# Four changes in the order of ScalarE's work in a fused attention and RG-LRU step

## The chip, the cores and the metric

The kernel runs on one core of a Trainium2 chip. A core has five engines that each work through a queue of their own, in the order in which the program wrote it: TensorE (PE) multiplies matrices, VectorE (DVE) and ScalarE (ACT) work element by element, so does GpSimd (POOL), and SyncE (SP) starts DMAs. An engine that has to wait for another stands still, and so does everything queued behind that instruction. The metric is the device time of one execution in microseconds (us).

## The reference, cut to what matters

One layer with two groups of heads that read the same normalised and modulated input, for 128 context tokens and 1024 latent tokens (1152 columns in all), model width 1024:

```python
h = rms_norm(x, g_pre) * (1.0 + scale) + shift          # shift, scale, gate = silu(c) @ w_ada + b_ada
p = h @ w_in
q, k, v, g_att, x_lru, g_lru = jnp.split(p, SPLITS, axis=-1)
q, k = axial_rope(q), axial_rope(k)                      # latent tokens only
o = diff_attention(q, k_all, v_all, lam)                 # 8 heads, two softmax maps per head
att = (rms_norm(o, g_subln) * (1.0 - lam_init)) * jax.nn.silu(g_att)
u = centred_conv(x_lru, conv_w, conv_b)
hf = linear_scan(a_f, b_f, h0_f, False)                  # a, b from two gates of u
hb = linear_scan(a_b, b_b, h0_b, True)
lru = (hf + hb) * jax.nn.silu(g_lru)
out = jnp.concatenate([att, lru], axis=-1) @ w_out
x_new = x + gate * rms_norm(out, g_post)
```

It returns both new token sets, the new keys and values, and the final states of the recurrence. Inputs and outputs are fp32.

## The kernel before, in words

**How a product is made.** An fp32 product is three products of 16-bit (or reduced fp32) halves, lines 119 to 121: high by high, low by high, high by low. Whatever TensorE multiplies must first be split: a cast or a scaled copy on ScalarE makes the high half, and an operation on VectorE (or GpSimd) subtracts it from the original and leaves the low half. For weights these are `whi` (line 314, ScalarE) and `wlo` (line 324, VectorE), for the input `hTh` (line 495) and `hTl` (line 116), for a head's queries and keys `hlq` and `hlk` (lines 931 and 932), for values lines 1021 and 1022, for the output weights `woh` (line 222, ScalarE) and `wol` (line 113, half of them on VectorE and half on GpSimd). Before a tensor is split it is scaled by a power of two; for a weight block that is `wunit` (squares on ScalarE at line 290, a sum over the partitions by TensorE at line 297, the power of two by VectorE at lines 194 to 199), and for a head `qksc` (squares on ScalarE at line 907, the sum by TensorE at line 918, the power of two at line 194 again).

**The stages.** Up to about 82 us the modulation is computed: sixteen pieces of `w_ada` in four groups A, B, C, D of four. `mod` multiplies one piece (line 434), `mod_rows` copies a group's result to SBUF on ScalarE (line 439), and `mod_turn` transposes it on TensorE (line 444). Groups A and B give scale and shift for the first half of the model's width (tiles 0 to 3 of the eight tiles of x), C and D for the second half (tiles 4 to 7). `unit_h`, `scales`, `bounds` and `shares` are small VectorE operations that make the factors `sc` and `sh` of a half. `normed` multiplies a tile by its norm (line 483), `modulate` applies scale and shift and casts to `hTh` (lines 492 and 495 on ScalarE; with `hi=V` lines 489 and 497 on VectorE), `h_lo` makes `hTl`. The first block of `w_in` is multiplied while this goes on: `first_chunk(k)` for tiles 0 to 3 into one set of accumulators, tiles 4 to 7 into another (`x0b`). From 82 to 410 us eight blocks of the recurrence run, from 410 to 706 us the heads' queries, keys and values with their gates, from 706 to 730 us the last gates, and from there to the end attention, with the products by `w_out` (`po`) between its tiles.

**What sets the order.** Each engine's order is the order in which the code was written. Blocks of heads are written by `qk_block` (line 897): for each of three column chunks `j` the product and its copy to SBUF on ScalarE (`qk_chunk`, line 764), and then `tick()`. `after(n, step)` puts a step off by n ticks, so that the later steps of one head (`power`, the sum and power of two; `turned`, the rotary embedding on VectorE at lines 891 to 894; `halves`, lines 931 and 932; `send`, the DMAs) are written between the chunks of the next. `squares` (line 907) is not put off: it is written behind the tick of the last chunk. `v_block` does the same for values; its copies are at line 983 and its halves at line 1021. `g_block` (line 1096 on) writes a gate: three chunks, three sigmoids (line 732), three products (line 738). The last gate is that of head 7. Four pieces of `w_out` and their splits are put off to ticks inside it; the second four loads into the same four buffers (`wor`) are put off too.

Of the kernel before, what the change touches and what calls it, by code (L numbers as in the profile page):

```python
# [29 lines left out]
NCH = T // CH  # L30
# [67 lines left out]
def hybrid_step_kernel(ctx: ExitStack, tc: tile.TileContext, io):  # L98
# [148 lines left out]
    with ExitStack() as pa:  # L247
# [118 lines left out]
        with ExitStack() as stp:  # L366
# [10 lines left out]

            xt = [sp.tile([P, T], F32, name=f"xt{k}") for k in range(KT)]
            what = {"A": (0, 1), "B": (0, 0), "C": (1, 1), "D": (1, 0)}
            for x in "A0 A1 w A2 A3 x0 x1 B0 x2 x3 B1 x4 x5 B2 x6 x7 B3 C0 C1 C2 C3 D0 D1 D2 D3 w w w".split():  # L380
                if x == "w":
                    w_load()
                elif x[0] == "x":
                    k = int(x[1])
                    nc.sync.dma_start(out=xt[k], in_=io["xT"][:, k])
                else:
                    load_wa(*what[x[0]], int(x[1]))
# [43 lines left out]
            def mod(half, part, b):  # L431
                raw = wa.pop((half, part, b))
                for i in range(2):
                    PE.matmul(modps[half, part][0:2], lhsT=cs[:, 2 * b + i], rhs=raw[:, i], start=b == 0 and i == 0,
                              stop=b == 3 and i == 1)

            def mod_rows(half, part):
                rows = modr[half, part] = sw.tile([2, 512], F32, tag="rows", name=f"rows{half}{part}", bufs=2)
                S.copy(out=rows, in_=modps[half, part][0:2])

            def mod_turn(half, part):
                t4 = ssq[:, 16:24].rearrange("p (i c) -> p i c", i=4)
                for i in range(4):
                    PE.transpose(t4[:, i], modr[half, part][:, i * P:(i + 1) * P], ident[0:2, 0:2])
                kk = part * 8 + half * 4
                V.tensor_tensor(out=modT[:, kk:kk + 4], in0=t4,
                                in1=vec[:, ba + kk:ba + kk + 4].unsqueeze(2).to_broadcast([P, 4, 2]), op=ALU.add)
# [38 lines left out]
            def modulate(k, eng=V, hi=S):  # L486
                for w, a, b in ((1, 0, CTX), (0, CTX, T)):
                    if eng is V:
                        V.tensor_scalar(out=xt[k][:, a:b], in0=xt[k][:, a:b], scalar1=sc1[:, w, k:k + 1],
                                        scalar2=sh1[:, w, k:k + 1], op0=ALU.mult, op1=ALU.add)  # L490
                    else:
                        S.activation(out=xt[k][:, a:b], in_=xt[k][:, a:b], func=AF.Identity, scale=sc1[:, w, k:k + 1],
                                     bias=sh1[:, w, k:k + 1])
                if hi is S:
                    S.copy(out=hTh[k], in_=xt[k])
                else:
                    V.tensor_copy(out=hTh[k], in_=xt[k])

            def h_lo(k):
                split_lo16(V, hTl[k], xt[k], hTh[k])  # L500
# [42 lines left out]
            normed(1)  # L543
            modulate(0, S)
            mod(*C, 3)
            modulate(1, S)
            normed(2)
            h_lo(0)
            mod_rows(*C)
            normed(3)  # L550
            mod(*D_, 0)
            modulate(2, S)
            h_lo(1)
            mod_turn(*C)
            for b in range(1, 4):
                mod(*D_, b)
            normed(4)
            modulate(3, S)
# [12 lines left out]
                for j in range(NCH):  # L571
                    chunk(accs[j] if k < 4 else accb[:, j], 16, 0, j, [k], k % 4 == 0, k % 4 == 3)

            for k in range(2):
                first_chunk(k)
            mod_turn(*D_)
            scales(1)
            bounds(1)
            unit_h(1)
            shares()  # L580
            for k in range(2, 4):
                first_chunk(k)
            modulate(4, S)
            modulate(6, hi=V)
            h_lo(6)
            w_back(1)
            h_lo(4)
            modulate(5, S)
            one = w_hi()
            modulate(7, hi=V)  # L590
            h_lo(7)
            h_lo(5)
            w_lo(one)
            for x, k in enumerate((4, 6, 7, 5)):
                for j in range(NCH):
                    chunk(accb[:, j], 16, 0, j, [k], x == 0, x == 3)
            w_square()
# [299 lines left out]
        def qk_block(which, h):  # L897
# [52 lines left out]
            if not first:  # L950
                for j in range(NCH):
                    qk_chunk(which, h, t_, j)
                    tick()
            if which or h > 1:
                squares()
                if which:
                    after(1, context_keys)
                for x, step in zip((1, 1, 3, 4), steps[1:]):
                    after(x, step)
            else:  # L960

                for x, step in zip(((5, 7, 8, 10, 11), (7, 9, 10, 12, 13))[h], steps):
                    after(x - 3 * h, step)
# [159 lines left out]
        load_lt(0, 0)  # L1123
        for kt in GROUPS[0]:
            load_wo(kt, 0)
        after(2, lambda: [split_wo(kt, 0, V if kt % 2 else G) for kt in GROUPS[0][:2]])
        after(3, lambda: [split_wo(kt, 0, V if kt % 2 else G) for kt in GROUPS[0][2:]])
        after(3, lambda: [load_wo(kt, 1) for kt in GROUPS[0]])
        assert len(AMONG) + 2 == NH
        g_block(gp_, NH - 1)  # L1130
        for n in range(2, 4):
            load_q(n)
        for t in range(1, 3):
# [569 lines left out]
```

## Time and profile before

| | |
|---|---|
| three runs | 1256.38, 1257.6, 1251.76 us; median 1256.38 us |
| profiled execution | 1255.92 us, span of its trace 1254.1 us |
| TensorE busy | 1141.9 us, 91% of the span |
| VectorE busy | 1033.5 us, 82% |
| ScalarE busy | 786.9 us, 63% |
| GpSimd busy | 302.1 us, 24% |
| chain that ended last, by engine | VectorE 36%, TensorE 36%, ScalarE 10%, DMA 7%, issue 7%, GpSimd 3% |

The span is the stretch that the trace covers; the execution's own time is 1.82 us longer. "Busy" counts time in which at least one instruction of the engine ran, so a product that runs at half clock counts for more. The chain is followed back from the last instruction: at each step to what released it.

### The profile page before, as it was taken

The numbers are of one execution on the slowest core, as the hardware profiler recorded it, in microseconds if no ns is written. First come the engines' busy times: TensorE is split into PE (matmuls) and PEld (weight loads), VectorE is DVE, ScalarE is ACT, GpSimd is POOL, SyncE is SP. The second block draws the span as 40 slices with busy tenths as digits, with TensorE's granted clock in tenths as the row PEclk, the third lists the DMA queues.
The fourth block names the chain that finished last, engine by engine and source line by source line (L and its number), as shares of the span: only waits on it lengthen the run. The fifth ranks groups of instructions, "written<-read, shape, count | busy, mean of one in ns | idle before, by whom it ended". The sixth has DMA issues, their size and how long they took to land.

```text
span 1254.1 us, 20667 instructions
## 1 busy us (share of the span) xinstructions
PE 1141.9 (91%) x7804; PEld 786.2 (63%) x7804; DVE 1033.5 (82%) x1880; ACT 786.9 (63%) x1330; POOL 302.1 (24%) x172
## 2 busy tenths in 40 slices
PE   6889999999999899899899969988989888999887
PEld 1346666666666755675766747766767665666675
DVE  5686898889887988867868547899898989999877
ACT  4457577657766555545445347877877786777632
POOL 0000000000000000000000013346965686667624
PEclk8889999999999999899899989999999999999999
DMA  9311322231223345625534276999888998899954
GB/s 363 142 43 43 116 70 73 91 116 61 81 91 105 98 116 172 167 73 151 152 102 91 78 242 133 212 207 231 189 209 187 230 225 176 200 205 223 197 205 159
DMA packets 277819, 188.76 MB, mean 151 GB/s; under 512 B 196172, under 2 KB 246092, under 8 KB 276952
## 3 DMA queue, kind: packets, MB, share of 16 engines
q1 hardware_dynamic: 277432, 186.60, 56.1%
q8 instruction: 61, 1.00, 0.3%
q10 hardware_dynamic: 288, 0.85, 0.2%
q14 instruction: 38, 0.31, 0.1%
HBM read 102.20 MB, written 46.94 MB: 119 GB/s over the span
## 4 chain that ended last, share of the span: by engine, by line
DVE 36%; PE 36%; ACT 10%; DMA 7%; issue 7%; POOL 3%; SPq 1%; DVEq 0%; ACTq 0%; POOLq 0%
DVE mx L1231 6%; DVE e L1259 5%; DVE wlo L324 3%; PE s L1222 2%; PE s L1224 2%; PE ga L119 2%; POOL a L1263 2%; PE v L119 2%; PE v L120 2%; PE v L121 2%; PE ga L120 2%; PE ga L121 2%; ACT e L1241 2%; PE po L119 2%; PE po L120 1%
## 5 line engine op out<-in xcount | busy, mean ns | idle before, releaser
L1241 ACT ACTIVATE e<-s,mx,back 128x1152 f32<-128x1152 f32 (+1 forms) x144 | 175.5, 1219 | 64.6 <-DVE mx L1237 16.9
L113 POOL TENSOR_TENSOR wol<-wor,woh 128x512 fp32r<-128x512 f32 x24 | 33.4, 1393 | 683.9 <-ACT woh L222 683.8
L1263 POOL TENSOR_TENSOR a<-e,a 128x1152 f16<-128x1152 f32 (+1 forms) x72 | 157.9, 2193 | 166.6 <-ACT a L1262 158.3
L1231 DVE TENSOR_REDUCE mx<-s 128x1 f32<-128x1152 f32 (+1 forms) x144 | 177.3, 1231 | 21.0 <-PE s L1224 20.1
L119 PEld LDWEIGHTS <-whi 128*128 128x128 f16 x960 | 96.6, 101 | 63.6 <-issue 6.4
L121 PEld LDWEIGHTS <-wlo 128*128 128x128 f16 x960 | 94.1, 98 | 65.4 <-issue 3.7
L120 PEld LDWEIGHTS <-whi 128*128 128x128 f16 x960 | 94.2, 98 | 64.1 <-issue 7.2
L1222 PE MATMUL s<-kt,qt 128*128 128x384 f16 (+1 forms) x400 | 88.0, 324 | 42.4 <-ACT e L1241 40.4
L1259 DVE SCALAR_TENSOR_TENSOR e<-e,fa,e 128x1152 f32<-128x1152 f32 (+1 forms) x72 | 114.3, 1587 | 6.4
L119 PE MATMUL po<-woh,lt 128*128 128x512 f32 x216 | 98.7, 457 | 12.8 <-DVE sg L738 7.1
L119 PE MATMUL pv<-vt,t 128*128 128x128 f16 x584 | 103.2, 221 | 3.1 <-ACT ot L1278 2.5
L120 PE MATMUL pv<-vt,t 128*128 128x128 f16 x584 | 102.7, 220 | 0.0
L121 PE MATMUL pv<-vt,t 128*128 128x128 f16 x584 | 102.6, 220 | 0.0
L1262 ACT CAST a<-e 128x1152 f16<-128x1152 f32 (+1 forms) x72 | 75.8, 1053 | 37.1 <-DVE e L1259 23.9
L1224 PE MATMUL s<-kt,qt 128*128 128x384 f16 (+1 forms) x400 | 87.8, 325 | 0.0
L121 PE MATMUL po<-woh,lt 128*128 128x512 f32 x216 | 86.3, 400 | 0.0
L120 PE MATMUL po<-wol,lt 128*128 128x512 f32 x216 | 85.8, 397 | 0.0
L119 PE MATMUL v<-whi,hTh 128*128 128x256 f16 x288 | 81.6, 283 | 3.2 <-DVE qksc L194 2.3
L120 PE MATMUL v<-wlo,hTh 128*128 128x256 f16 x288 | 81.6, 283 | 0.0
L121 PE MATMUL v<-whi,hTl 128*128 128x256 f16 x288 | 81.4, 282 | 0.0
L1222 PEld LDWEIGHTS <-qt 128*128 128x128 f16 x400 | 33.6, 97 | 71.4 <-issue 59.3
L324 DVE SCALAR_TENSOR_TENSOR wlo<-wraw,wboth,whi 128x512 f16<-128x512 f32 x94 | 66.2, 746 | 12.7 <-ACT whi L314 12.4
(361 smaller groups left out, 3242.7 us busy)
## 6 DMA issues: line engine op xcount, KB each, us to landing
wraw<-in_w_in_dram SPq DMA_DIRECT2D x48, 512.0 KB, 3.6
lt<-mix SPq DMA_DIRECT2D x27, 512.0 KB, 4.1
qs<-hlq SPq DMA_DIRECT2D x64, 144.0 KB, 3.1
qt<-qs SPq DMA_DIRECT2D x72, 128.0 KB, 3.5
wa<-in_w_ada_dram SPq DMA_DIRECT2D x16, 512.0 KB, 10.6
wor<-in_w_out_dram SPq DMA_DIRECT2D x32, 256.0 KB, 3.7
mix<-amo SPq DMA_DIRECT2D x6, 1152.0 KB, 5.8
vs<-v SPq DMA_DIRECT2D x8, 640.0 KB, 2.9
```

Of the source, the lines that this page charges most:

```text
L113: eng.tensor_tensor(out=lo, in0=val, in1=f(hi), op=ALU.subtract)
L119: PE.matmul(out, lhsT=lh, rhs=rh, start=start, stop=False)
L120: PE.matmul(out, lhsT=lh, rhs=rl, start=False, stop=False)
L121: PE.matmul(out, lhsT=ll, rhs=rh, start=False, stop=stop)
L324: V.scalar_tensor_tensor(out=lo[:, i % 2, r], in0=raws[i][:, r], scalar=wboth[:, i, x:x + 1], in1=hi[:, i % 2, r], op0=ALU.mult, op1=ALU.s ...
L1222: PE.matmul(sps[:, j, :w_], lhsT=qt[:, mp], rhs=kt_[:, mp, c], start=True, stop=False)
L1224: PE.matmul(sps[:, j, :w_], lhsT=qt[:, 2 + mp], rhs=kt_[:, mp, c], start=False, stop=True)
L1231: V.tensor_reduce(out=d["mx"][:, mp:mp + 1], in_=sv, axis=AX.XY, op=ALU.max, negate=True)
L1241: S.activation(out=e_[:, :nk].rearrange("p (j c) -> p j c", c=w_), in_=sv, func=AF.Exp, bias=d["mx"][:, mp:mp + 1], scale=unit, accum_out= ...
L1259: V.scalar_tensor_tensor(out=e1, in0=e1, scalar=d["fa"], in1=e0, op0=ALU.mult, op1=ALU.subtract)
L1262: S.copy(out=a16[:, 0:nk], in_=e1)
L1263: G.tensor_tensor(out=a16[:, nk:2 * nk], in0=e1, in1=a16[:, 0:nk], op=ALU.subtract)
```

## The change

Four things are written in another order, and one cast changes its engine.

- The DMAs of x and of group B's weights: each of B1, B2 and B3 is ahead of one tile of x more than before, and B0 ahead of x1.
- Before the first block: group C's rows are copied ahead of `modulate(1)`, not behind it; `mod(D,1)` stands ahead of C's transpose on TensorE; only tile 0's chunk stands ahead of D's transpose (tiles 0 and 1 before); tile 6 is written ahead of tile 4, the cast of tile 7 moves from VectorE to ScalarE, and the chunks of the second half run in the order 6, 4, 7, 5.
- Squares of a head: `squares` is called between the last chunk's copy and its tick, which is ahead of whatever that tick writes: the halves of the head before, or of two values.
- The last gate: the splits of the first four pieces of `w_out` and the loads of the second four are written behind the gate's sigmoids and products.

```diff
--- before.py
+++ after.py
@@ -377,7 +377,7 @@
 
             xt = [sp.tile([P, T], F32, name=f"xt{k}") for k in range(KT)]
             what = {"A": (0, 1), "B": (0, 0), "C": (1, 1), "D": (1, 0)}
-            for x in "A0 A1 w A2 A3 x0 x1 B0 x2 x3 B1 x4 x5 B2 x6 x7 B3 C0 C1 C2 C3 D0 D1 D2 D3 w w w".split():
+            for x in "A0 A1 w A2 A3 x0 B0 x1 x2 B1 x3 x4 B2 x5 x6 B3 x7 C0 C1 C2 C3 D0 D1 D2 D3 w w w".split():
                 if x == "w":
                     w_load()
                 elif x[0] == "x":
@@ -543,16 +543,17 @@
             normed(1)
             modulate(0, S)
             mod(*C, 3)
+            mod_rows(*C)
             modulate(1, S)
             normed(2)
             h_lo(0)
-            mod_rows(*C)
             normed(3)
             mod(*D_, 0)
             modulate(2, S)
             h_lo(1)
+            mod(*D_, 1)
             mod_turn(*C)
-            for b in range(1, 4):
+            for b in range(2, 4):
                 mod(*D_, b)
             normed(4)
             modulate(3, S)
@@ -571,27 +572,26 @@
                 for j in range(NCH):
                     chunk(accs[j] if k < 4 else accb[:, j], 16, 0, j, [k], k % 4 == 0, k % 4 == 3)
 
-            for k in range(2):
-                first_chunk(k)
+            first_chunk(0)
             mod_turn(*D_)
             scales(1)
             bounds(1)
             unit_h(1)
             shares()
-            for k in range(2, 4):
+            for k in range(1, 4):
                 first_chunk(k)
+            modulate(6, hi=V)
             modulate(4, S)
-            modulate(6, hi=V)
             h_lo(6)
-            w_back(1)
+            modulate(7)
             h_lo(4)
             modulate(5, S)
+            w_back(1)
+            h_lo(7)
             one = w_hi()
-            modulate(7, hi=V)
-            h_lo(7)
             h_lo(5)
             w_lo(one)
-            for x, k in enumerate((4, 6, 7, 5)):
+            for x, k in enumerate((6, 4, 7, 5)):
                 for j in range(NCH):
                     chunk(accb[:, j], 16, 0, j, [k], x == 0, x == 3)
             w_square()
@@ -950,9 +950,10 @@
             if not first:
                 for j in range(NCH):
                     qk_chunk(which, h, t_, j)
+                    if j == NCH - 1 and (which or h > 1):
+                        squares()
                     tick()
             if which or h > 1:
-                squares()
                 if which:
                     after(1, context_keys)
                 for x, step in zip((1, 1, 3, 4), steps[1:]):
@@ -1123,11 +1124,12 @@
         load_lt(0, 0)
         for kt in GROUPS[0]:
             load_wo(kt, 0)
-        after(2, lambda: [split_wo(kt, 0, V if kt % 2 else G) for kt in GROUPS[0][:2]])
-        after(3, lambda: [split_wo(kt, 0, V if kt % 2 else G) for kt in GROUPS[0][2:]])
-        after(3, lambda: [load_wo(kt, 1) for kt in GROUPS[0]])
         assert len(AMONG) + 2 == NH
         g_block(gp_, NH - 1)
+        for kt in GROUPS[0]:
+            split_wo(kt, 0, V if kt % 2 else G)
+        for kt in GROUPS[0]:
+            load_wo(kt, 1)
         for n in range(2, 4):
             load_q(n)
         for t in range(1, 3):
```

ScalarE before the first block, the difference (`rows` is the copy of a modulation group, `hTh` the cast high half of a tile, numbers are buffers):

```order
 L495 CAST hTh_131<-xt_157 128x1152
+L439 COPY rows_383<-modpA 2x512
 L492 ACTIVATE xt_158<-xt_158,sh_117,sc_116 128x128
 L492 ACTIVATE xt_158<-xt_158,sh_117,sc_116 128x1024
 L495 CAST hTh_132<-xt_158 128x1152
-L439 COPY rows_388<-modpA 2x512
 L492 ACTIVATE xt_159<-xt_159,sh_117,sc_116 128x128
 L492 ACTIVATE xt_159<-xt_159,sh_117,sc_116 128x1024
```

The copy of group C's rows has moved up past one tile's two activations and its cast. Further down the queue the cast of tile 7 has come in between the cast of tile 4 and the activations of tile 5.

ScalarE at the end of a key block, before (`qfk_4584` is the block just multiplied, `qfk_4458` the one before it, `wjunk` the squares):

```order
L764 ACTIVATE qfk_4584<-k_1_4667,winv 128x384
L764 ACTIVATE qfk_4584<-k_2_4693,winv 128x384
L931 ACTIVATE hlk_4719<-qfk_4458,qksc 128x1280
L907 ACTIVATE wjunk,sqk_4722<-qfk_4584 128x1280
L983 ACTIVATE vf_0_4724<-v_0_4729,winv 128x128
```

and the same place now:

```order
L764 ACTIVATE qfk_4584<-k_1_4667,winv 128x384
L764 ACTIVATE qfk_4584<-k_2_4693,winv 128x384
L907 ACTIVATE wjunk,sqk_4719<-qfk_4584 128x1280
L931 ACTIVATE hlk_4721<-qfk_4458,qksc 128x1280
L984 ACTIVATE vf_0_4724<-v_0_4729,winv 128x128
```

The squares of the new block and the high half of the block before it have changed places; this happens at thirteen ends of blocks, and at three of them two value halves (line 1021, 1022 now) stand between as well.

ScalarE at the last gate, before (`woh` casts of `w_out`, `sg` the gate's sigmoids):

```order
L222 CAST woh_0_6925<-wor_0_6867 128x512
L222 CAST woh_0_6929<-wor_0_6869 128x512
L222 CAST woh_0_6958<-wor_0_6871 128x512
L222 CAST woh_0_6962<-wor_0_6873 128x512
L732 ACTIVATE sg_6974<-ga_0_6875,winv 128x384
L732 ACTIVATE sg_6974<-ga_1_6900,winv 128x384
L732 ACTIVATE sg_6974<-ga_2_6933,winv 128x384
L222 CAST woh_1_6991<-wor_1_6966 128x512
L222 CAST woh_1_6995<-wor_1_6968 128x512
```

and now:

```order
L732 ACTIVATE sg_6950<-ga_0_6875,winv 128x384
L732 ACTIVATE sg_6950<-ga_1_6900,winv 128x384
L732 ACTIVATE sg_6950<-ga_2_6925,winv 128x384
L222 CAST woh_0_6957<-wor_0_6867 128x512
L222 CAST woh_0_6961<-wor_0_6869 128x512
L222 CAST woh_0_6965<-wor_0_6871 128x512
L222 CAST woh_0_6969<-wor_0_6873 128x512
L222 CAST woh_1_6991<-wor_1_6973 128x512
L222 CAST woh_1_6995<-wor_1_6975 128x512
```

The three sigmoids stand ahead of the first four casts; the second four casts stay where they were behind them. On VectorE the gate's three products have moved up past two `wol` in the same way.

## Rows read from the trace of the kernel before

**Rows 1.** Stretches: us, busy PE, PEld, DVE, ACT, POOL (instructions), PE clock, DMA share, GB/s.

```profile
0.00:45.00 45.00, 35.09 (x100) 9.75 (x100) 23.35 (x73) 16.74 (x19) 1.05 (x11) 0.89 0.93 352
45.00:82.00 37.00, 28.01 (x123) 12.74 (x122) 29.41 (x63) 22.98 (x32) 0.34 (x6) 0.82 0.04 15
82.00:410.00 328.00, 324.31 (x1982) 213.73 (x1981) 279.21 (x435) 224.07 (x286) 0.00 (x0) 1.00 0.26 83
```

**Rows 2.** TensorE before first block: start, duration, operation, [idle <-releaser].

```profile
49.42 0.58 PE L444 MATMUL ssq<-ident,rows 2*128 2x2 f32 x4 [3.95 <-ACT rows L439]
...
69.46 0.48 PE L120 MATMUL x0b<-hTl,whi 128*128 128x384 f16 x1 [2.58 <-DVE hTl L116]
...
77.86 0.28 PE L297 MATMUL ssq<-wsq,onesf 128*128 128x1 f32 x2
```

**Rows 3.** ScalarE before the first block.

```profile
57.55 0.57 ACT L439 COPY rows<-modpB 2x512 f32<-2x512 f32 x1 [1.71 <-PE modpB L434]
63.70 1.63 ACT L492 ACTIVATE xt<-xt,sh,sc 128x128 f32<-128x128 f32 x2 [5.57 <-DVE sh L471]
65.35 1.15 ACT L495 CAST hTh<-xt 128x1152 f16<-128x1152 f32 x1
```

**Rows 4.** VectorE before the first block.

```profile
64.50 1.06 DVE L489 TENSOR_SCALAR xt<-xt,sc,sh 128x128 f32<-128x128 f32 x2
65.60 0.76 DVE L497 CAST hTh<-xt 128x1152 f16<-128x1152 f32 x1
66.39 1.36 DVE L116 TENSOR_TENSOR hTl<-xt,hTh 128x1152 f16<-128x1152 f32 x1
```

**Rows 5.** Three stretches at half clock, columns as in rows 1.

```profile
68.19:75.02 6.83, 5.56 (x18) 2.60 (x18) 6.76 (x8) 4.45 (x7) 0.00 (x0) 0.50 0.00 0
522.16:528.99 6.83, 6.04 (x29) 4.42 (x30) 6.16 (x22) 3.93 (x11) 0.00 (x0) 0.50 0.42 126
733.79:740.61 6.82, 3.10 (x7) 2.48 (x8) 4.75 (x6) 4.50 (x9) 3.81 (x3) 0.50 0.74 232
```

**Rows 6.** Who waited for the squares of line 907 (us, times).

```profile
  PE unk L918: 9.8, 3
```

**Rows 7.** TensorE at two kinds of pause among the heads.

```profile
522.95 0.58 PE L918 MATMUL unk<-sqk,onesf 128*128 128x1 f32 x2 [4.28 <-ACT wjunk L907]
...
591.28 0.32 PE L119 MATMUL k<-hTh,whi 128*128 128x384 f16 x1 [1.75 <-DVE wunit L194]
```

**Rows 8.** ScalarE ahead of the first of these pauses.

```profile
520.28 1.36 ACT L931 ACTIVATE hlk<-qfk,qksc 128x1280 f16<-128x1280 f32 x1 [3.90 <-DVE qfk L894]
521.55 1.25 ACT L907 ACTIVATE wjunk<-qfk 128x1280 bf16<-128x1280 f32 x1
```

**Rows 9.** One round of two blocks, columns as in rows 1.

```profile
518.50:589.50 71.00, 66.42 (x459) 46.34 (x458) 53.36 (x124) 35.67 (x65) 0.00 (x0) 0.95 0.40 119
```

**Rows 10.** VectorE in that round, first and last of five such pauses.

```profile
542.57 0.54 DVE L973 TENSOR_REDUCE vmx<-vf 128x1 f32<-128x128 f32 x2 [0.80 <-ACT vf L983]
...
555.60 0.16 DVE L1013 COPY sgv<-vmu 128x2 f32<-128x2 f32 x1 [0.59 <-PE vmu L1012]
```

**Rows 11.** TensorE between last gate and attention.

```profile
737.51 0.79 PE L119 MATMUL po<-woh,lt 128*128 128x512 f32 x1 [7.05 <-DVE sg L738]
...
743.34 0.65 PE L1222 MATMUL s<-kt,qt 128*128 128x384 f16 x3 [1.24 <-ACT e L1241]
```

**Rows 12.** ScalarE there.

```profile
730.51 1.32 ACT L222 CAST woh<-wor 128x512 fp32r<-128x512 f32 x2 [10.14 <-DMA wor<-in_w_out_dram]
...
734.58 1.51 ACT L732 ACTIVATE sg<-ga,winv 128x384 f32<-128x384 f32 x3
...
741.44 1.28 ACT L1241 ACT_TABLE_LOAD   x1 [1.82 <-DVE mx L1234]
```

**Rows 13.** VectorE there.

```profile
735.80 1.66 DVE L738 SCALAR_TENSOR_TENSOR sg<-ga,winv,sg 128x384 f32<-128x384 f32 x3
```

## The prediction

> **What bounds the kernel now.** I read the page's busy shares first, and then one row for each stage, because no engine is the bound throughout. From 82 to 410 us TensorE is busy for 324.31 of 328.00 us [rows 1]: what comes earlier into that stage leaves it earlier by as much, and nothing there is touched. Before it, from 45 to 82 us, TensorE is busy for 28.01 of 37.00 us at a mean clock of 0.82, so pauses and slow products are both to be had. I then looked in TensorE's timeline for pauses that end on ScalarE or on something that ScalarE holds up. There are three kinds in the places that the change touches. Before the first block TensorE waits 3.95 us for the copy of group C's rows and later 2.58 us for the low half of a tile [rows 2]. Among the heads it waits for the squares: 9.8 us in three pauses for keys [rows 6], one of them 4.28 us at 522.95 [rows 7]. Between the last gate and attention it waits 7.05 us for the gate's products [rows 11].
>
> A pause costs more than its length. The granted clock is 0.50, which is 1.2 GHz of 2.4, from 522.16 to 528.99 around the end of the 4.28 us pause, and from 733.79 to 740.61 at the end of the 7.05 us one [rows 5]. A pause of the second kind, shorter and ended by VectorE, is that at 591.28: 1.75 us for the power of two of a weight block [rows 7].
>
> **The change part by part.**
>
> *Loads.* Three pieces of B come one tile of x (128 x 1152 fp32, 0.59 MB) earlier. At the 352 GB/s of the first 45 us [rows 1] that is 1.7 us, and it can't help by more; at worst, since the tiles of x come later by a piece of B (0.52 MB), it costs 1.5 us. What follows needs both, so most of it cancels; I take −0.4 us.
>
> *Modulation.* The copy of group C's rows passes one tile's activations and cast, 1.63 and 1.15 us [rows 3], and a piece of D stands ahead of the transpose, so the pause of 3.95 us goes. What is late next is ScalarE itself: the copy of D's rows waited 1.71 us for TensorE [rows 3], so this copy can come 1.71 us earlier and no more. Behind it only tile 0's nine products stand ahead of D's transpose. At half clock 18 products of this shape took 5.56 us [rows 5], so nine take 2.8 us, and at full clock 1.4 us. I count the half clock here, and let the factors of the second half of the model's width be ready 1.35 us earlier than at 63.70 [rows 3], that is at 62.35.
>
> *Second half.* VectorE's queue decides from there. It began 0.80 us after the factors (64.50 against 63.70) [rows 3, 4]. Now it has tile 6's modulation and cast, tile 7's modulation, and four low halves: 1.06 + 0.76 + 1.06 + 4 x 1.36 = 8.3 us [rows 4], with about 1.3 us for the weight's small operations and hand-overs. The last low half is there at 62.35 + 0.80 + 8.3 + 1.3 = 72.8 us, and the nine products behind it end at 74.2 if the clock is full. Before, the step behind these products began at 77.86 [rows 2]: −3.6 us. The cast of tile 7 leaves VectorE's queue and costs ScalarE 1.15 us [rows 3], beside work of VectorE. If the clock falls, all 36 products of the half take twice as long, and if ScalarE's extra cast delays tile 5, another 1.15 us is lost, so the ends are −5 and 0.
>
> The Trainium skill (ScalarE: Activation LUTs, section Rules for kernel authors) says that simple elementwise work belongs on VectorE, which is faster at it; the rows agree, 0.76 against 1.15 us, and by the rule the move of the cast would lose 0.4 us. By the rows it takes 0.76 us out of the queue that decides here.
>
> *Squares.* At thirteen block ends the squares (1.25 us, [rows 8]) pass the halves of the block before. At 520.28 ScalarE had stood still for 3.90 us ahead of those halves, because it waited for the rotary embedding on VectorE, with the squares queued behind [rows 8]. So the squares fill idle time, the halves aren't late there, and the pause of 4.28 us goes. With all three such pauses gone that is −9.8 us [rows 6], and the half clock behind two of them costs half of up to 6.04 us of products each [rows 5]: −15.8 us is the lower end. But VectorE, in order, can't follow so far. In the round of 71.00 us from 518.5 it is busy for 53.36 us [rows 9], and of its 17.6 us idle only five pauses, from 542.57 to 555.60, end on products or their copies; they add to 5.4 us [rows 10]. The others end on halves that follow its own rotary embedding, and don't shrink. TensorE then comes earlier to the weight of the next block and waits there: the 1.75 us at 591.28 [rows 7] grow to some 4. I take −4 us for this round. The next round of the same make has no more than its half us to give, since VectorE enters it with that slack used up: −4.5 us in all. The upper end is 0: everything that the squares gave back is waited for at weights.
>
> *Last gate.* The three sigmoids (1.51 us) stood behind four casts that waited for loads, 10.14 us [rows 12]; they can now begin when TensorE has ended the gate's last product, at 730.46 (737.51 less the 7.05 us of its pause) [rows 11], 4 us earlier than 734.58. Then the gate's products on VectorE (1.66 us, [rows 13]) and the first products by `w_out` come some 5 us earlier than 737.51 [rows 11]. What is late next is the chain that this doesn't shorten: loads, casts and low halves of eight pieces, and behind them in the same queues the scores' first maximum and the table load at 741.44 [rows 12]. The second four loads still need the first four buffers. So the scores at 743.34 [rows 11] stay where they are, TensorE stands still for some 6 us before them in place of 1.24, and its first products run at half clock, as they did from 733.79 [rows 5]: half of 3.10 us busy is 1.5 us, of which some is hidden; I take +1.0 us. At best the waits of 1.82 and 1.24 us at 741.44 and 743.34 go as well (−3.1); at worst the second loads come later by the sigmoids and products that now go first (+3.2), and the clock costs 1.5: +4.7.
>
> *Sum.* −0.4 − 3.6 − 4.5 + 1.0 = −7.5 us. The profiled execution took 1255.92 us (span 1254.1 and 1.8 us around it), 0.46 us under the median of the three runs: 1248.4 us. Attention, behind 745 us, is the same work in the same order and only shifts.
>
> **The rivals.**
>
> *All pauses go.* VectorE's order turns out to have the slack, TensorE stays at full clock through the heads: −12 us there in place of −4.5, with the rest as above, 1240.9 us, between 1238 and 1244. For it: VectorE is busy for only 53.36 of 71.00 us [rows 9]. Against it: the pause at 591.28 already ends on VectorE [rows 7].
>
> *The pauses move.* TensorE gains at the squares and loses the same at the weights: pauses like that at 591.28 grow from 1.75 to over 4 us, as long as the ones before which the clock fell [rows 5, 7], and the half clock returns at these places. Then the heads give 0, and the prologue half of its 4.0: 1255.92 − 2.0 + 1.0 = 1254.9 us, between 1252 and 1258. That the reordering does nothing where it counts ends here too.
>
> By the Trainium skill (TensorE: Matmul & The Clock Gate, section HAM oscillation) a kernel whose matrix engine pauses again and again pays half of each throttled stretch anew. Here that would be half of 6.83 us behind each pause that comes back [rows 5], and the trace agrees so far.
>
> *Slower.* The squares delay the halves. Where ScalarE is not idle ahead of them, above all at the three places with two value halves, each of thirteen places makes a half, the low half on VectorE and the next rotary embedding 1.25 us later [rows 8]. If VectorE's queue is the bound through all heads, that is +16.3 us, less 4.0 of the prologue and with 1.0 of the gate: 1269 us. It ends above 1262.7 us from eight places on (8 x 1.25 = 10.0). Against it are the 3.90 us of idle time at 520.28.
>
> **How the numbers follow.** Chances: the forecast 0.50 (own range 1244 to 1253), all pauses go 0.17, the pauses move 0.26, slower 0.07. About 0.5% (6.3 us) is what a measurement of this kernel can tell from no change, so faster means below 1250.1 us: all of the first rival and 0.36 of the forecast's 0.50, 0.53. Within 0.5%: the forecast's other 0.14 and 0.26, 0.40. Slower 0.07. The range leaves out the lower part of the first rival, the upper part of the second and the third: 1239.5 to 1257.
>
> **What would show it.** Right: no pause over 1 us on group C's rows; the step at 77.86 some 4 us earlier; the pause of 4.28 us for the squares gone, and waits for VectorE's power of two before the later key blocks that are longer than 1.75 us; the first product by `w_out` 5 us earlier against the rest, with a new pause of about 6 us ahead of the scores. Wrong would be a TensorE that stays at full clock from 410 to 706 us (the first rival), a stretch of the heads as long as before with the half clock at other places (the second), or a VectorE that waits longer for halves than for products (the third).

## The result and the profile after

The changed kernel took 1246.32 us in the median of five runs (1245.74 to 1247.83), the kernel before 1256.38 us (five runs, 1251.76 to 1257.6). The ratio is 0.9928, 95% interval 0.9908 to 0.9948: 0.7% faster. That is 10.1 us between the medians and 9.0 us (6.5 to 11.6) by the ratio. 1248.4 us with a range of 1239.5 to 1257.0 had been forecast, 7.5 us less than the kernel before. The span of the profiled execution fell from 1254.1 to 1244.5 us.

First the page of the changed kernel: busy time by engine, and TensorE's granted clock in 40 slices.

```profile
PE 1138.2 (91%) x7804; PEld 784.2 (63%) x7804; DVE 1029.8 (83%) x1879; ACT 788.9 (63%) x1331; POOL 304.5 (24%) x172
...
PEclk8899999999999999999999989999999999999999
```

TensorE and VectorE are busy for 3.7 us less each (1141.9 and 1033.5 before), the span is 9.6 us shorter: so 5.9 of the 9.6 us are time in which TensorE stood still. The stretches ahead of the heads, columns as in [rows 1]:

```profile
0.00:45.00 45.00, 34.84 (x95) 10.13 (x96) 21.26 (x71) 15.23 (x17) 1.05 (x11) 0.85 0.93 352
45.00:82.00 37.00, 28.52 (x139) 13.49 (x137) 32.39 (x71) 26.77 (x37) 0.34 (x6) 0.95 0.08 26
82.00:410.00 328.00, 324.53 (x1989) 214.35 (x1988) 279.44 (x434) 224.81 (x285) 0.00 (x0) 1.00 0.26 83
```

From 45 to 82 us the mean clock is 0.95 where it was 0.82, but from 0 to 45 it is 0.85 where it was 0.89 [rows 1]. TensorE's timeline of the changed kernel shows both, answering to [rows 2]:

```profile
41.78 2.27 PE L540 MATMUL rb<-ident,yc 128*128 128x128 f32 x18
...
49.23 0.41 PE L444 MATMUL ssq<-ident,rows 2*128 2x2 f32 x4
...
58.01 0.58 PE L297 MATMUL ssq<-wsq,onesf 128*128 128x1 f32 x2 [4.85 <-ACT wjunk L290]
...
76.09 0.28 PE L297 MATMUL ssq<-wsq,onesf 128*128 128x1 f32 x2
...
77.10 0.32 PE L119 MATMUL g<-hTh,whi 128*128 128x384 f16 x1
```

The transpose of group C at 49.23 waits for nothing any more (3.95 us before). A new pause of 4.85 us stands at 58.01, ahead of the sum of a weight's squares: TensorE has run out of work earlier and waits for ScalarE. The step that stood at 77.86 is at 76.09.

Among the heads, TensorE's pauses, answering to [rows 7], and ScalarE at the first of the old pauses, answering to [rows 8]:

```profile
520.21 0.27 PE L119 MATMUL v<-whi,hTh 128*128 128x256 f16 x1 [1.91 <-ACT vf L984]
...
583.18 0.32 PE L119 MATMUL k<-hTh,whi 128*128 128x384 f16 x1 [2.42 <-ACT qfk L764]
...
663.42 0.32 PE L119 MATMUL k<-hTh,whi 128*128 128x384 f16 x1 [2.77 <-ACT qfk L764]
```

```profile
513.29 1.27 ACT L907 ACTIVATE wjunk<-qfk 128x1280 bf16<-128x1280 f32 x1
...
518.29 1.36 ACT L931 ACTIVATE hlk<-qfk,qksc 128x1280 f16<-128x1280 f32 x1 [3.64 <-DVE qfk L894]
```

The squares run at 513.29, in what was idle time, and ScalarE then waits 3.64 us for the rotary embedding with the squares no longer queued behind. TensorE's pause of 4.28 us is gone. A pause of 1.91 us for the copies of the values stands behind it, and the weight pauses are now 2.42 and 2.77 us, ended by copies of keys. For all squares TensorE now waits 2.4 us (1.6 for queries and 0.8 for keys), where keys alone cost 9.8 [rows 6] and queries another 2.5.

VectorE's five pauses of 5.4 us on products and copies in this round [rows 10] have shrunk to one, and in the next round TensorE waits for VectorE at a place where it did not wait before, the transpose of the values' maxima:

```profile
547.53 0.16 DVE L1014 COPY sgv<-vmu 128x2 f32<-128x2 f32 x1 [0.38 <-PE vmu L1013]
```

```profile
622.78 0.27 PE L1003 MATMUL vmt<-ident,vm 128*2 128x128 f32 x1 [1.80 <-DVE vm L996]
```

This second pause stands in the traces of all ten kernels in which squares were moved (1.80 to 2.57 us), and in none of the three that have them in the old order and nothing filled in (before, e3, e10).

At the last gate, TensorE's two pauses (answering to [rows 11]), and VectorE's queue between them:

```profile
721.27 0.51 PE L119 MATMUL po<-woh,lt 128*128 128x512 f32 x1 [1.07 <-ACT woh L222]
...
733.53 1.12 PE L1224 MATMUL s<-kt,qt 128*128 128x384 f16 x3 [6.15 <-ACT e L1243]
```

```profile
729.86 1.19 DVE L113 TENSOR_TENSOR wol<-wor,woh 128x512 fp32r<-128x512 f32 x1 [1.71 <-ACT woh L222]
730.98 0.28 DVE L1233 TENSOR_REDUCE mx<-s 128x1 f32<-128x128 f32 x1
```

The pause of 7.05 us ahead of the first product by `w_out` has become 1.07, and the one of 1.24 us ahead of the scores has become 6.15. The scores' first maximum at 730.98 stands behind the last `wol`, as it did in the kernel before:

```profile
739.65 1.20 DVE L113 TENSOR_TENSOR wol<-wor,woh 128x512 fp32r<-128x512 f32 x1 [1.15 <-ACT woh L222]
740.77 0.28 DVE L1231 TENSOR_REDUCE mx<-s 128x1 f32<-128x128 f32 x1
```

To compare kernels, each trace was read at three places: when the second block's first product begins (`g`, line 119), how long the heads take (from the first value product, 408.82 in the kernel before, to the end of the gate's products, which is where the pause ahead of the first `po` begins), and from there to the scores of the second tile (743.34 in the kernel before). Each trace is of one execution, and not always of a middling one: e1's (1252.56 us) is the slowest of its six, f3's (1240.47 us) the fastest of its six. All kernels that follow are in the table; "13" and "2" are the places at which squares stand ahead of the halves.

| kernel | before first block | squares | gate | `g` begins | heads | gate to scores |
|---|---|---|---|---|---|---|
| before | old | old | old | 78.70 | 321.6 | 12.9 |
| e10_prologue | new | old | old | 75.18 | 321.8 | 12.5 |
| e3_gate | old | old | new | 78.28 | 321.8 | 12.4 |
| e2_squares | old | 13 | old | 77.43 | 315.6 | 12.0 |
| e6_two_squares | old | 2 | old | 78.63 | 313.9 | 11.6 |
| f4_fill | old | old, filled | old | 78.87 | 318.4 | 12.6 |
| changed | new | 13 | new | 77.10 | 313.2 | 13.3 |
| f1, changed again | new | 13 | new | 73.63 | 316.2 | 12.5 |
| e1_old_loads | new but loads | 13 | new | 76.50 | 319.2 | 12.8 |
| e4_late_splits | new | 13 | late | 74.35 | 316.0 | 7.6 |
| e8_lt_first | new | 13 | late | 74.86 | 316.3 | 7.8 |
| e9_chunks_first | new, chunks | 13 | new | 73.38 | 315.6 | 12.7 |
| f2_prologue_two | new | 2 | old | 73.14 | 314.5 | 12.4 |
| f3, with chunks | new, chunks | 2 | old | 73.50 | 315.0 | 12.3 |

### The profile page after: what moved, and what is told of

Its sections match the earlier page's. It is cut to its first block, busy times and chain, and to the rows that moved or that the text cites. A ratio compares the mean times of both kernels' runs of the same rounds, so it can differ in the third digit from the quotient of the medians.

```text
span 1244.5 us, 20662 instructions
## 1 busy us (share of the span) xinstructions
PE 1138.2 (91%) x7804; PEld 784.2 (63%) x7804; DVE 1029.8 (83%) x1879; ACT 788.9 (63%) x1331; POOL 304.5 (24%) x172
## 4 chain that ended last, share of the span: by engine, by line
DVE 42%; PE 27%; ACT 11%; issue 8%; DMA 7%; POOL 4%; SPq 1%; DVEq 0%; ACTq 0%; POOLq 0%
DVE mx L1233 6%; DVE e L1261 4%; DVE wlo L324 4%; DMA t<-a 3%; POOL a L1265 2%; PE ga L119 2%; ACT e L1243 2%; PE ga L120 2%; PE s L1224 2%; PE ga L121 2%; PE s L1226 2%; PE x L119 1%; PE x L121 1%; PE x L120 1%; PE po L119 1%
## 5 line engine op out<-in xcount | busy, mean ns | idle before, releaser
L119 PE MATMUL v<-whi,hTh 128*128 128x256 f16 x288 | 78.5, 272 | 5.4 <-DVE qksc L194 2.3
L121 PE MATMUL v<-whi,hTl 128*128 128x256 f16 x288 | 78.5, 273 | 0.0
L120 PE MATMUL v<-wlo,hTh 128*128 128x256 f16 x288 | 78.5, 272 | 0.0
```

The source lines that it names most:

```text
L119: PE.matmul(out, lhsT=lh, rhs=rh, start=start, stop=False)
L120: PE.matmul(out, lhsT=lh, rhs=rl, start=False, stop=False)
L121: PE.matmul(out, lhsT=ll, rhs=rh, start=False, stop=stop)
```

## The experiments

The kernel before was run again beside each set: 1258.24 us (18 runs), 1256.33 (29) and 1255.63 (17). Its executions spread from 1250 to 1263 us, so ratios are against the runs of the same set.

### The order ahead of the first block: e1, e10, f1

The first profile of the changed kernel had gained only 1.6 us at `g`, and its norm's broadcast (41.78) came 2.1 us later than before. My first theory was the loads. e1 undoes them alone:

```diff
-            for x in "A0 A1 w A2 A3 x0 B0 x1 x2 B1 x3 x4 B2 x5 x6 B3 x7 C0 ...
+            for x in "A0 A1 w A2 A3 x0 x1 B0 x2 x3 B1 x4 x5 B2 x6 x7 B3 C0 ...
```

> The changed kernel with the old order of the loads of x and B; all else as changed. Theory 1 (the new load order cost the prologue its gain: it turned TensorE's waits into one of 2.96 us ahead of A's transpose, and C1 and C2 then ran at half clock from 34.08 to 40.90 in place of 34.05 to 37.47): the norm's broadcast products begin near 39.7 as before (41.78 in the changed kernel), the step behind the second half's products comes near 74.8 in place of 76.9, and the time falls by some 2 us to about 1244.3. Rival (the half clock there comes with any order, or the loads gave 0.4 us as forecast): the same 41.8, and 1246 to 1247 us.

Measured: 1247.93 us (ratio 0.9925, 0.990 to 0.995), the broadcast at 41.22. The theory fell: the late broadcast comes with the old loads too. e10 takes the whole part alone:

> The kernel before with the loads and the order ahead of the first block changed, squares and last gate as before. My forecast for this part was 4.0 us, the profiles of two kernels with the same part show 1.6 and 4.35 us at the first product of the second block, and what they differ in is where the half clock lay. Theory 1 (4 us on the mean over executions): 1254 us against 1258. Rival (the half clock takes most of it): 1257.

Measured: 1252.58 us, ratio 0.9972 (0.9952 to 0.9993). So this part gives 3.5 us, between 0.9 and 6.0. f1 is the changed kernel again:

> The changed kernel once more, beside the others of this set. Its first profile had the first product of the second block at 77.10 and the heads' stretch (first value product to the gate's last product) at 313.2 us; kernels with the same code there showed 74.35 to 75.2 and 315.3 to 316. If those spreads are executions and not code, this profile differs from the first by one to three us at either place; the median stays between 1245 and 1248.

Measured: 1245.05 us (0.9915, 0.9888 to 0.9941), the broadcast at 37.93 and `g` at 73.63, 3.5 us earlier than in the first profile of the same program, and the heads took 316.2 us, some 3 us longer. (The 315.3 of the expectation is e4's, counted from a product 0.7 us behind the first one; counted from the first, as in the table, it is 316.0.) One stretch of the first profile and of the second:

```profile
30.00:42.00 12.00, 11.74 (x38) 4.47 (x36) 4.95 (x27) 0.26 (x1) 0.00 (x0) 0.69 1.04 396
```

```profile
30.00:42.00 12.00, 11.74 (x59) 5.81 (x57) 6.37 (x29) 0.37 (x1) 0.00 (x0) 1.00 1.04 395
```

TensorE is busy for 11.74 us in both, with 38 instructions at a mean clock of 0.69 in the first and 59 at 1.00 in the second. Nothing in the program differs. The clock fell at other places, and the broadcast came 3.9 us earlier. The broadcast in f1, and in the kernel before:

```profile
37.93 2.27 PE L540 MATMUL rb<-ident,yc 128*128 128x128 f32 x18
```

```profile
39.67 2.27 PE L540 MATMUL rb<-ident,yc 128*128 128x128 f32 x18
```

Counted from the broadcast, most of the spread is gone: `g` begins 38.45 to 39.30 us behind it in the five traces with the old order, and 35.27 to 35.72 us behind it in the nine with the new one (35.32 in the first profile, 35.70 in f1). The new order gives 3.5 us on the mean in this stretch, and all nine traces are ahead of all five. What the loads give can't be told: the broadcast itself came between 37.42 and 41.78 us in the eight traces with the new loads, between 38.13 and 41.22 in the six with the old.

### The squares: e2, e6, f4

e2 has the squares of the change alone.

> The kernel before with the squares alone moved ahead of the halves. Theory 1 (the heads gave 8.4 us, of which some 2.3 are pauses and the rest products no longer at half clock): 1248 us, span some 8 us shorter than 1254.1, no half clock behind the third key and fifth key blocks, pauses of 1.8 to 2.8 us for copies and weights in their place. Rival (my forecast: VectorE takes back all but 4.5 us): about 1252 us. Rival 2 (the heads' gain needs the prologue's shift of time against the clock): 1252 or more, with half-clock stretches at the new pauses.

Measured: 1250.77 us, ratio 0.9948 (0.9926 to 0.9971), which is 6.5 us. The heads took 315.6 us against 321.6 to 321.8 in the three kernels with the old order. The clock does not fall at 522 or 604, but at 623.38 and 664.34, for 3.41 us each, and the pauses are those of the changed kernel (1.91, 2.41, 2.78 us). e6 moves them at two places:

```diff
                     qk_chunk(which, h, t_, j)
+                    if j == NCH - 1 and which and h in (3, 5):
+                        squares()
                     tick()
             if which or h > 1:
-                squares()
+                if not (which and h in (3, 5)):
+                    squares()
```

> The kernel before with the squares moved at two of the thirteen places alone, the key blocks of heads 3 and 5, which ended on the pauses of 4.28 and 4.08 us. Theory 1 (what the squares gave is these two pauses and the half clock behind each; the other eleven places were about free): most of what all thirteen gave (7.5 us between the medians, 6 us in the trace from the first gap to the last gate), so 1251 to 1253 us against 1258, no half clock at 522 and 604. Rival (the many short pauses and the later blocks share the gain evenly): two thirteenths, about 1257 us.

Measured: 1250.31 us, ratio 0.9948 (0.9926 to 0.9969), as much as all thirteen. Its heads took 313.9 us. TensorE and one stretch of e6:

```profile
522.66 0.27 PE L119 MATMUL v<-whi,hTh 128*128 128x256 f16 x1 [0.78 <-ACT vf L986]
...
585.66 0.32 PE L119 MATMUL k<-hTh,whi 128*128 128x384 f16 x1 [1.75 <-DVE wunit L194]
```

```profile
522.00:529.00 7.00, 6.27 (x57) 5.47 (x56) 6.53 (x22) 4.10 (x12) 0.00 (x0) 1.00 0.42 123
```

The pause for the values' copies is 0.78 us where it is 1.91 with thirteen, and the weight pause stays at 1.75. The full clock holds across the stretch that was at 0.50 [rows 5]; it falls once, for 3.41 us from 586.95, behind the pause of 1.75 us.

f4 leaves the wait as it was in the kernel before and fills the two long pauses with products that nothing reads.

```diff
                 tp = small(f"un{name}")
+                if which and h in (3, 5):
+                    for _ in range(24):
+                        PE.matmul(tp[:, :CH], lhsT=hTh[0][:, :P], rhs=hTh[0][:, :CH], start=True, stop=True)
                 PE.matmul(tp[:, 0:1], lhsT=onesf, rhs=d["sq"], start=True, stop=True)
```

> The kernel before with 24 products whose result nothing reads put into each of the two pauses of 4.28 and 4.08 us, ahead of the sum over the squares (3.9 us at full clock each): the wait for the squares stays, TensorE doesn't stand still in it. Theory 1 (a good part of the two squares' gain is the half clock behind the pauses): no half clock at 522 and 604, and 2 to 4 us of the 6 us come back, 1252 to 1254 against 1256 to 1258. Rival (it was the pauses' own length, and the clock costs nothing since VectorE decides next): 1256 to 1258, no change.

Measured: 1255.53 us, ratio 0.9998 (0.9978 to 1.0017): no difference in the times. In its trace TensorE and the stretch behind the first pause read:

```profile
518.72 4.06 PE L920 MATMUL unk<-hTh 128*128 128x384 f16 x24
523.14 0.38 PE L921 MATMUL unk<-sqk,onesf 128*128 128x1 f32 x2 [0.35 <-ACT wjunk L907]
```

```profile
523.00:530.00 7.00, 6.86 (x63) 6.18 (x64) 6.33 (x22) 4.26 (x12) 0.00 (x0) 1.00 0.52 164
```

The sum starts at the same place behind the block as before and the clock behind it is 1.00. Between two sums of weights (line 297), behind head 3's key block and ahead of the pause at 591.28, the kernel before took 70.55 us (518.22 to 588.77), f4 67.61, e2 65.10, the changed kernel 65.11 and e6 64.47. By these traces 2.9 of the 5.4 us that the squares gave in this round are the clock, which is half of the 6.04 us of products at half clock [rows 5], and 2.5 the shorter pause. The times don't confirm it for the whole program: the interval allows f4 a gain of 2.8 us at most, where its heads are 3.3 us shorter in one trace. In the round behind it f4 is hardly shorter (95.53 against 95.81 us up to the weight sum at 684.58), though the second pause was filled too. How much of the time the clock makes is left open.

### The last gate: e3, e4, e8

e3 has this part of the change alone.

> The kernel before with the last gate alone put ahead of the casts of w_out. Theory 1 (the pause only moves, from 7.05 us ahead of the first product by w_out to some 6 us ahead of the scores; the traces show +0.45 us over the stretch): 1256 to 1257 us against 1256.4, no difference that can be measured. Rival (the first products by w_out come 5 us earlier and attention follows): about 1252 us.

Measured: 1257.68 us, ratio 0.9995 (0.9978 to 1.0012): nothing. TensorE in e3:

```profile
731.48 0.47 PE L119 MATMUL po<-woh,lt 128*128 128x512 f32 x1 [1.26 <-ACT woh L222]
...
742.60 0.80 PE L1223 MATMUL s<-kt,qt 128*128 128x384 f16 x2 [5.45 <-ACT e L1242]
```

The pause has moved as in the changed kernel. e4 takes the chain away that holds the scores, by putting the second four splits behind the first two tiles of attention:

```diff
         load_v(0)
-        for kt in GROUPS[0]:
-            split_wo(kt, 1, V if kt % 2 else G)
         tick()
...
+        for x in range(2):
+            at_period(x, lambda x=x: [split_wo(kt, 1, V if kt % 2 else G) for kt in GROUPS[0][2 * x:2 * x + 2]])
```

> The changed kernel with the splits of the second four pieces of w_out moved behind the first two tiles of attention, two behind each. Theory 1 (the 6.15 us pause ahead of the scores is the chain of those splits on ScalarE and VectorE, and nothing else holds the first maximum): the pause shrinks to under 2 us, attention starts some 4 to 6 us earlier and the time falls to about 1242. Rival (the loads or the table load hold it, or attention, where VectorE is busy for nine tenths, pays the splits' 2.4 us and more back): 1245 to 1247 us.

Measured: 1245.05 us (0.9898, 0.9873 to 0.9922). This is the lowest ratio of all, but its interval overlaps that of the changed kernel (0.9908 to 0.9948), which did not run in this set. The scores come 5.8 us earlier, but the profiled span is 1244.8 us, no shorter than the changed kernel's: from the scores to the end it is 517.0 us where the changed kernel has 511.0. TensorE in e4:

```profile
727.77 0.65 PE L1222 MATMUL s<-kt,qt 128*128 128x384 f16 x3 [0.59 <-ACT e L1241]
...
733.09 0.50 PE L119 MATMUL po<-woh,lt 128*128 128x512 f32 x1 [3.20 <-DMA lt<-mix]
```

The pause of 6.15 us is 0.59, and one of 3.20 us has come for a load that had been queued behind those of the second four pieces. e8 puts that load ahead of them:

```diff
-        for kt in GROUPS[0]:
-            load_wo(kt, 1)
         for n in range(2, 4):
             load_q(n)
         for t in range(1, 3):
             load_lt(0, t)
+        for kt in GROUPS[0]:
+            load_wo(kt, 1)
```

> The kernel with the late splits (second four pieces of w_out split behind the first two tiles), and the next queries' and attention inputs' loads put ahead of the second four pieces' loads on SyncE. There TensorE had waited 3.20 us at 733.09 for such a load. Theory 1 (the 5.8 us that the late splits gave at the scores were given back at that load and at two splits among the scores): the pause at 733 goes and the time falls by another 2 to 3 us, to about 1242.5. Rival (VectorE decides in attention, the load only covered it): 1245, no change against the late splits alone.

Measured: 1247.46 us (0.9928, 0.9901 to 0.9954), no better. TensorE in e8:

```profile
735.24 0.65 PE L1222 MATMUL s<-kt,qt 128*128 128x384 f16 x3 [1.56 <-ACT e L1241]
...
739.03 0.80 PE L119 MATMUL po<-woh,lt 128*128 128x512 f32 x1 [2.66 <-ACT acc L1182]
```

The wait for the load is gone, and 1.56 and 2.66 us of waits for ScalarE stand in its place; from the scores to the end it is 516.9 us. The rival holds by these traces: in the other twelve the stretch from the scores to the end takes 508.0 to 513.1 us, so the five microseconds that e4 and e8 win at the start of attention are given back in it. The times allow e4 a gain of a few microseconds, which e8 does not repeat.

### Towards a faster version: e9, f2, f3

e9 lets TensorE run two chunks in its new pause of 4.85 us.

```diff
             normed(6)
-            w_unit(ssq)
             normed(7)
...
             first_chunk(0)
+            first_chunk(1)
+            w_unit(ssq)
             mod_turn(*D_)
...
-            for k in range(1, 4):
+            for k in range(2, 4):
```

> The changed kernel with the weight unit's sum on TensorE (w_unit) put behind the first two chunks of the first block. In the changed kernel TensorE stood still for 4.85 us ahead of it for ScalarE's squares, and the first chunk ran behind it. Theory 1 (this pause is the place where the removed 3.95 us pause of group C went): the 4.85 us shrink to under 2, D's transpose comes 1.5 to 3 us earlier and the first block with it; 1244 to 1245 us. Rival (the copy of D's rows on ScalarE, at the same time as before, decides): 1246 to 1247 us.

Measured: 1246.47 us (0.9932, 0.9911 to 0.9952). TensorE in e9:

```profile
54.30 0.38 PE L297 MATMUL ssq<-wsq,onesf 128*128 128x1 f32 x2 [1.82 <-ACT wjunk L290]
57.34 0.56 PE L444 MATMUL ssq<-ident,rows 2*128 2x2 f32 x4 [2.65 <-DVE wunit L194]
```

The pause is 1.82 us, but D's transpose now waits 2.65 for VectorE. `g` at 73.38 is within what the same order reached without it (73.14 to 77.10), and 35.31 us behind the broadcast, as there.

> The order ahead of the first block as changed, the squares moved at the two places alone (key blocks of heads 3 and 5), the last gate as before. Theory 1 (two places give all that the squares give, the gate gives nothing): as fast as the changed kernel or 1 to 2 us faster, 1244 to 1247. Rival (the eleven other places and the gate each hold a part): 1249 or more.

Measured: 1244.96 us (0.9911, 0.9884 to 0.9937), beside 1245.05 for the changed kernel in the same set. Eleven of the thirteen places and the gate's part are worth nothing that can be measured in these runs. f3 is f2 with e9's edit.

> The same with the weight unit's sum on TensorE behind the first two chunks. Theory 1 (D's transpose comes 1.5 us earlier): 1 to 2 us under the kernel without it. Rival (ScalarE's copy of D's rows decides): the same.

Measured: 1244.61 us (0.9913, 0.9885 to 0.9941): the same. None of these versions is faster than the changed kernel by more than the runs can tell.

## Why the prediction was right

The sign, the size and the path held. Forecast were −7.5 us; measured are −10.1 between the medians and −9.0 by the ratio, whose interval (−6.5 to −11.6) contains the forecast. Part by part the traces give −3.5 for the order ahead of the first block, −5.7 for the squares and +0.4 for the gate, −8.8 in all. The squares' term is the one furthest from its forecast (−4.5), though the interval of its own run, −3.6 to −9.3, contains it.

*Ahead of the first block*, forecast −4.0 us (0.4 for loads, 3.6 for the order). Measured alone: −3.5 us (−0.9 to −6.0), and on the mean of traces `g` at 74.71 (six with the new order) against 78.38 (five with the old): −3.7. The changed kernel's own profile shows only 1.6, because its broadcast came late. Counted from the broadcast, the working can be followed step by step: the copy of D's rows came 1.7 us earlier (16.08 against 17.79 us on the mean; "1.71 us earlier and no more"), the factors 1.15 us earlier (1.35 forecast), the step behind the second half's products 3.7 us earlier (3.6 forecast). The pause of 3.95 us turned into the 4.85 us one on ScalarE. The loads' 0.4 can't be told from nothing.

*Squares*, forecast −4.5 us, measured −6.5 alone (−3.6 to −9.3); in the traces the heads took 316.0 us on the mean of seven kernels with thirteen places against 321.7, −5.7. TensorE's sums of weights mark the rounds, in the kernel before and in the changed one:

```profile
518.22 0.28 PE L297 MATMUL wu<-wsq,onesf 128*128 128x1 f32 x2
...
588.77 0.28 PE L297 MATMUL wu<-wsq,onesf 128*128 128x1 f32 x2
...
684.58 0.28 PE L297 MATMUL wu<-wsq,onesf 128*128 128x1 f32 x2
```

```profile
515.09 0.28 PE L297 MATMUL wu<-wsq,onesf 128*128 128x1 f32 x2
...
580.20 0.28 PE L297 MATMUL wu<-wsq,onesf 128*128 128x1 f32 x2
...
674.32 0.28 PE L297 MATMUL wu<-wsq,onesf 128*128 128x1 f32 x2
```

I had read VectorE's five pauses on products as a limit of 5.4 us for the first round, and taken 4. It gave 5.4 to 5.5 in all seven traces with thirteen places, and in the changed kernel the five pauses are down to one of 0.38 us; but two places alone gave 6.1, so 5.4 is not a strict limit. The second round, up to 684.58, I gave half a microsecond, "since VectorE enters it with that slack used up". It gave 1.7 in the changed kernel's first trace, and was 0.7 to 2.1 us longer in the six others (96.6 on the mean of seven against 95.81). Up to the weight sum at 670.92 it looks 1.3 to 2.7 us shorter in all seven, but the pause for a copy of keys, now 2.77 us and sometimes with the half clock, stands just behind that sum. The step held: TensorE now waits there for VectorE (1.80 us at 622.78), and the half clock is back in some traces. Both rounds together gave 4.7 us on the mean. That this comes so close to the 4.5 forecast is luck: the first gave 1.4 more than was taken, the second 1.3 less. What the sum left at nothing is the third pause for keys, 1.49 us at 471.32: ahead of 518.22 six of the seven traces are 1.3 us shorter (e1, with a half-clock stretch there, is 1.0 longer). The pause at the weight came out smaller than I had it and ended otherwise: not some 4 us for VectorE's power of two, but 2.42 (and 2.77) us for a copy of keys on ScalarE, and with two places it did not grow at all. That sign of the prediction failed.

*Last gate*, forecast +1.0 us: +0.4 on the mean of traces (12.7 against 12.3), nothing in the times. "The scores at 743.34 stay where they are" was right against the gate's end, with the pause of 6 us ahead of them (6.15).

*The rivals.* That all pauses go is refuted: new ones of 1.8 to 2.8 us stand in their place, and the heads gave 5.7 us, not 12. Its sign nearly came all the same: between 410 and 706 us the changed kernel's first trace is at half clock only once, for 3.41 us; f1 is so four times. That the pauses move is half true, and its price was wrong: the moved pauses are shorter than those they replace. The rule of the Trainium skill (TensorE: Matmul & The Clock Gate, section HAM oscillation) that each renewed pause pays half of a throttled stretch agrees for the 4.28 us pause in the one trace that shows it: the round is 2.9 us shorter in f4, where the pause was filled. Behind the pauses that replaced the two long ones it holds in part: two stretches of 6.83 us at half clock became one of 3.41 in the changed kernel (from 583.62), three of 3.41 in f1, and in e1 one of 3.41 and one of 6.83:

```profile
664.88:671.71 6.83, 5.84 (x19) 2.81 (x19) 6.45 (x20) 1.61 (x5) 0.00 (x0) 0.50 0.72 159
```

Slower is refuted: VectorE lost nothing by squares at thirteen places that a total could show, though two places alone had shorter heads (314.5 on the mean of three traces, against 316.0).

## What to carry to other kernels

In an engine that works in order, look for the instruction with an early input and a waiting reader that is queued behind one with a late input; where that is so, exchange them there, and only there: two places out of thirteen gave as much as all. A wait that stands ahead of a stage with another bound (here the scores ahead of attention) can come back inside the stage when you take it away. When you cut a trace into stretches, put the cut behind the pause that may have moved, or you count a gain that is given back just after it. And before an unexpected stretch of one profile is explained, profile the same program twice, and count from an event behind the part that varies.

## What the runs showed of the hardware

The same program had `g` begin at 77.10 in one execution and at 73.63 in another, with the granted clock at 0.50 in other places. For the kernel before all executions lie between 1249.98 and 1262.7 us, for the changed one between 1243.47 and 1247.83.

The pauses of 4.28 and some 4.1 us among the heads each went with 6.83 us at half clock that began within the pause, in the three traces that had them unfilled (before, e3, e10). The pause of 1.9 us that replaced the first went with none in all seven traces that have it. The pauses of 2.4 to 2.8 us that end on copies of keys went with none in some traces, with 3.41 us in others, and one of 2.77 us, in e1, with 6.83. A pause of 1.75 us at a weight went with none in the kernel before (591.28) and was followed by 3.41 us in e6 (from 586.95). So in this range the length of the pause alone does not tell whether the clock falls.
